# Convolution read from PSUM pairs, a one-engine solver, ordered norm products and separate weight buffers in a two-layer kernel

## The chip, the core and the metric

The kernel runs on one core of a Trainium2 chip. The metric is device time in microseconds (us) of one execution, the median of several. TensorE (PE) multiplies matrices and writes its results to PSUM, which has eight banks of 128 x 512 float32. ScalarE (ACT) and VectorE (DVE) read PSUM and SBUF; in this kernel GpSimd (POOL) works on SBUF alone, and all transfers are issued on the queue of SyncE (SP). Each engine takes its instructions in the order in which they stand in its queue and waits at the first one that is not ready.

## What is computed

Two layers, one after the other, on 1024 tokens of width 1024. The first layer normalizes x, projects it, and runs two branches: neighbourhood attention on a 16 x 64 grid (8 heads of 64), and a gated delta rule in chunks (4 heads of 128, forwards and backwards). The branch of the delta rule begins with a depthwise convolution of five taps over the tokens, and each chunk needs a triangular solve:

```python
qkv = jax.nn.silu(_centred_depthwise_conv(jnp.concatenate([dq, dk, dv], axis=-1), conv_w))
...
a_mat = jnp.where(strict, jnp.einsum('bhncd,bhnsd->bhncs', kb, k) * decay, 0.0) + jnp.eye(C)
sol = lax.linalg.triangular_solve(a_mat, rhs, left_side=True, lower=True, unit_diagonal=True)
...
y = jnp.einsum('ble,ed->bld', jnp.concatenate([attn, delta], axis=-1), w_out)
return x + y
```

The second layer normalizes again and runs stick-breaking attention (8 heads of 128) and a chunked retention (4 heads of 256), merges them through gates, and adds the result to its input.

## The kernel before, in words

Every large product is made three times, with a high and a low part of each operand (`fp32r`): hi x hi, lo x hi, hi x lo. `split_unit` loads 128 rows of a weight matrix into a `raw` buffer and makes the two parts, on POOL (L70 rounds, L71 subtracts), or, with `fast`, for every second unit on ACT (L67) and DVE (L68). `load_units` does so for the eight units of a product; ten `wu` buffers hold them. All units share three `raw` buffers.

PSUM is divided once for the whole program: three accumulators `a` (`psA`) and five banks `z` (two), `t`, `o` and `p` (`psB`). `dense_tok` (L102) makes products of 128 tokens, `dense_col` (L112) products of 128 columns in two accumulators of 512 tokens.

The program is written in this order. **Gates** (L238 to L290): a product for gates and `dz`, then a chain of small operations that ends in a transpose copied out as `growt` (L285). **Delta rule** (L298 to L433), for each of four heads `h`: the weights; for q, k and v (`b`) a `dense_col`, whose accumulators ACT copies to a padded SBUF tile `pad` (L309), after which DVE makes the five taps from `pad` (L312 once, L314 four times) and ACT the silu (L317); norms, transposes and copies (`kt`, `kT`, `vt`); decay matrices `E`; products `pkk` and `pkq`, multiplied by `E` into `N` (L400) and `IT` (L415), and scaled copies `sct` (L424, L428), all written to DRAM. When the last head's `N` is there, `X` (128 systems of 64 x 64, one to a partition) is read back (L433).

**Attention with the solver**: `na_proj(p)` projects q, k, v for a pair of heads (per 128 tokens: squares, a sum, a power on POOL at L126, three copies L495 to L497 on ACT, two scalings L500 on DVE), `na_attn(p)` runs eight steps of scores and values. For p = 0 and 1 the sixteen steps alternate with steps of `solver()`, which goes through 62 columns: for each it multiplies (L457) and adds (L459), on DVE for the rows from 8 up and on POOL for the rows below 8, and on DVE again for the last seven columns. `dz_raw` makes one more projection. For p = 2 the steps alternate with `merges`, which read the solver's result from DRAM; for p = 3 with the scan over chunks.

**Output and second norm**: `out_blocks` (L853) makes the output product in eight blocks of 128 columns for each of two sets of tokens (`s`); `residual` adds x (L860) and `square_sum` collects squares; `normalize(s)` multiplies the eight blocks by the norm (L911), casts (L912) and subtracts (L913). The products of set 0 are taken between the blocks of set 1. Nine `xo` buffers hold the blocks. **Stick-breaking attention** has eight heads with `fast` weights; its tiles lie in the pool `sr`, on the side of SBUF where `hp`, which holds the operand of `out_blocks`, lay.

A pool that is laid over a closed pool waits for all that used the old one. The order within each engine's queue isn't the written one: the builder plans it (`schedule_with_timeline_sim=True`) with its own durations, earlier statements first where both are ready. The order is fixed in the program.

Of the kernel before, what the change touches and what calls it, by code (L numbers as in the profile page):

```python
# [19 lines left out]
P = 128  # L20
# [16 lines left out]
def tile_kernel(ctx: ExitStack, tc: tile.TileContext, I: dict, out: bass.AP, dbg=None, stop=None):  # L37
# [10 lines left out]
    psA = ctx.enter_context(tc.tile_pool(name="psA", bufs=3, space=PSUM))  # L48
    psB = ctx.enter_context(tc.tile_pool(name="psB", bufs=1, space=PSUM))
# [11 lines left out]
    def split_unit(src, ncol, pool=None, tag="wu", parts=1, fast=False, rpool=None):  # L61
        raw = (rpool or wraw).tile([P, ncol], F32, tag="raw", name="raw", bufs=8 if rpool else 3)
# [11 lines left out]
    def load_units(w, c0, width, parts=1, stride=0, pool=None, tag="wu", fast=False, rpool=None):  # L74
        us = []
        for k in range(NK):
            rows = w[k * P:(k + 1) * P, :]
            if parts == 1:
                src = rows[:, c0:c0 + width]
            else:  # L80
                src = rows[:, c0:c0 + parts * stride].rearrange("p (g s) -> p g s", g=parts)[:, :, :width]
            us.append(split_unit(src, width * parts, pool, tag, parts, fast and k % 2 == 1, rpool))
        return us
# [3 lines left out]
    def bank(tag, w=512):  # L87
        if tag == "a":
            return psA.tile([P, w], F32, tag="a", name="acc")
        return psB.tile([P, w], F32, tag=tag, name="p" + tag, bufs=2 if tag == "z" else 1)  # L90
# [16 lines left out]
    def dense_col(hT, us, c0):  # L107
        accs = [bank("a") for _ in range(2)]
# [87 lines left out]


# [55 lines left out]
    onesPP = gp.tile([P, P], F32, name="onesPP")  # L253
    nc.vector.memset(onesPP, 1.0)
    trile = gp.tile([P, P], F32, name="trile")
    trige = gp.tile([P, P], F32, name="trige")
    nc.gpsimd.affine_select(out=trile, in_=onesPP, pattern=[[1, P]], compare_op=ALU.is_ge, fill=0.0, base=0, channel_multiplier=-1)
    nc.gpsimd.affine_select(out=trige, in_=onesPP, pattern=[[-1, P]], compare_op=ALU.is_ge, fill=0.0, base=0, channel_multiplier=1)

# [37 lines left out]
    dc = dc_.__enter__()  # L297
    for h in range(4):  # L298
        kt = dn.tile([P, NM, P], F32, tag="kt", name="kt")
        vt = dn.tile([P, NM, P], F32, tag="sct", name="vt", bufs=2)  # L300
# [3 lines left out]
        for b in range(3):  # L304
            pad = dc.tile([P, T + 4], F32, tag="pad", name="pad", bufs=2)
            nc.gpsimd.memset(pad[:, 0:2], 0.0)
            nc.gpsimd.memset(pad[:, T + 2:T + 4], 0.0)
            for half, acc in enumerate(dense_col(hT, us, b * P)):
                nc.scalar.copy(out=pad[:, 2 + half * 512:2 + half * 512 + 512], in_=acc)  # L309
            cv = dc.tile([P, T], F32, tag="cv", name="cv", bufs=2)  # L310
# [9 lines left out]
        sq = dc.tile([P, T], F32, tag="cv", name="sq", bufs=2)  # L320
# [40 lines left out]
        for d in range(2):  # L361
# [27 lines left out]
            else:  # L389
                E2 = decay(gb, G, 1, True, "E1")  # L390
                nc.vector.tensor_tensor(out=E2, in0=E2, in1=bb, op=ALU.mult)
                for g in range(2):
                    pkk = bank("t")
# [4 lines left out]
                    for dd_, E in enumerate((E0, E2)):  # L398
                        N = dn.tile([P, 4, P], F32, tag="IN", name="N", bufs=2)
# [7 lines left out]
                for g in range(2):  # L407
                    pkq = bank("p")
# [4 lines left out]
                    for dd_, E in enumerate((E0, E1)):  # L413
                        IT = dn.tile([P, 4, P], F32, tag="IN", name="IT", bufs=2)
# [4 lines left out]
        for d in range(2):  # L419
            dh, G = d * 4 + h, Gs[d]  # L420
            nc.scalar.activation(out=G, in_=G, func=AF.Exp)
            for f, src in enumerate((kT, sT[0])):
                sc_t = dn.tile([P, NM, P], F32, tag="sct", name="sct", bufs=2)
# [3 lines left out]
            sc_t = dn.tile([P, NM, P], F32, tag="sct", name="sct", bufs=2)  # L427
# [14 lines left out]

# [932 lines left out]
```

## Time and profile before

| | us |
|---|---|
| median of 3 runs | 2250.16 (2249.15 to 2255.03) |
| the profiled execution | 2252.17 |
| its span, first to last instruction | 2250.5 |
| PE busy | 2163.0 (96%) |
| POOL busy | 1105.4 (49%) |
| DVE busy | 1102.5 (49%) |
| ACT busy | 766.0 (34%) |

A matmul's busy time covers its pipeline, so two neighbours overlap and a busy PE may still wait a little. The profile also has the clock that PE was granted, as a share of full speed; its two levels are 1.2 and 2.4 GHz.

### The profile page before, as it was taken

Reading aid. Unit: us, or ns where it says so; the run is one execution under the profiler, and the core shown is the slowest. Engines: PE = TensorE matmul, PEld = TensorE weight load, DVE = VectorE, ACT = ScalarE, POOL = GpSimd, SP = SyncE. Lnnn points to the kernel's source line nnn. Section 1 sums busy time; section 2 is a strip of 40 time slices with the busy share of each in tenths; the row PEclk is TensorE's granted clock in tenths of the full one; section 3 lists DMA queues with packets and bytes.
Section 4 is the critical chain, followed back from the end, with each engine's and each line's share of the span. In section 5 each row is a group of like instructions: output and inputs, shape, how many; then the busy total and the mean of one; then the engine's idle time right before and its main releaser. Section 6 shows DMA issues by size and latency. Waiting matters only on the chain.

```text
span 2250.5 us, 33410 instructions
## 1 busy us (share of the span) xinstructions
PE 2163.0 (96%) x12325; PEld 1882.8 (84%) x12325; DVE 1102.5 (49%) x1980; ACT 766.0 (34%) x1912; POOL 1105.4 (49%) x1451
## 2 busy tenths in 40 slices
PE   7999888899999999999999999999999999999999
PEld 7777777787889878999999998888988888878887
DVE  4688879953446553566555655123333432231321
ACT  5354433445555322444333433112222322321200
POOL 6667777773101345344333334356565755354532
PEclk9999999899999999999999999999999999999999
DMA  4255740126377542111111112212333323564433
GB/s 132 83 152 157 206 129 26 36 82 190 90 278 246 176 130 63 41 61 57 57 42 34 43 57 71 89 58 79 107 94 120 126 92 114 179 227 159 146 109 106
DMA packets 240196, 250.27 MB, mean 111 GB/s; under 512 B 40161, under 2 KB 175521, under 8 KB 239777
## 3 DMA queue, kind: packets, MB, share of 16 engines
q1 hardware_dynamic: 240032, 248.14, 35.3%
q8 instruction: 97, 1.59, 0.3%
q14 instruction: 67, 0.54, 0.1%
HBM read 172.56 MB, written 75.53 MB: 110 GB/s over the span
## 4 chain that ended last, share of the span: by engine, by line
PE 68%; DVE 11%; POOL 6%; issue 5%; DMA 5%; ACT 2%; SPq 1%; POOLq 0%; DVEq 0%; ACTq 0%
PE acc L112 29%; PE acc L102 17%; PE acc L853 3%; PE po L1083 2%; PE pz L1051 2%; DVE X L459 2%; DVE svt L457 2%; POOL wu L71 2%; DVE cv L314 1%; POOL wu L70 1%; DMA raw<-in_w_in_dram 1%; PE pz L546 1%; PE pt L563 1%; POOL ss L126 1%; PE pp L577 1%
## 5 line engine op out<-in xcount | busy, mean ns | idle before, releaser
L112 PE MATMUL acc<-h2h,wu 128*128 128x512 f32 x1440 | 438.4, 393 | 0.7 <-ACT lg L958 0.7
L102 PE MATMUL acc<-wu,h2h 128*128 128x384 f32 (+1 forms) x1536 | 366.8, 322 | 6.6 <-ACT lg L972 2.2
L71 POOL TENSOR_TENSOR wu<-raw,wu 128x512 fp32r<-128x512 f32 (+3 forms) x276 | 366.3, 1335 | 7.2
L70 POOL TENSOR_SCALAR wu<-raw 128x512 fp32r<-128x512 f32 (+3 forms) x276 | 205.8, 749 | 313.0 <-PE acc L112 202.4
L112 PEld LDWEIGHTS acc<-h2h,wu 128*128 128x128 f32 x1440 | 269.5, 188 | 54.9 <-ACT lg L958 1.1
L102 PEld LDWEIGHTS acc<-wu,h2h 128*128 128x128 f32 x1536 | 265.8, 191 | 11.6 <-ACT lg L972 2.6
L112 PE MATMUL acc<-h2l,wu 128*128 128x512 f32 x720 | 265.2, 392 | 0.0
L102 PE MATMUL acc<-wu,h2l 128*128 128x384 f32 (+1 forms) x768 | 244.9, 321 | 0.0
L102 PE MATMUL acc<-wu,h1hi 128*128 128x384 f32 (+2 forms) x768 | 192.2, 334 | 11.1 <-DVE kS L512 5.2
L112 PE MATMUL acc<-h1hi,wu 128*128 128x512 f32 x512 | 167.3, 416 | 6.8 <-ACT pad L309 3.2
L125 POOL TENSOR_SCALAR ss<-ss 128x2 f32<-128x2 f32 (+2 forms) x136 | 36.7, 270 | 269.6 <-ACT sq L1001 215.0
L112 PEld LDWEIGHTS acc<-h2l,wu 128*128 128x128 f32 x720 | 135.0, 188 | 26.5
L102 PEld LDWEIGHTS acc<-wu,h1hi 128*128 128x128 f32 x768 | 137.0, 195 | 16.0 <-issue 6.5
L102 PEld LDWEIGHTS acc<-wu,h2l 128*128 128x128 f32 x768 | 146.1, 191 | 1.6
L112 PEld LDWEIGHTS acc<-h1hi,wu 128*128 128x128 f32 x512 | 100.4, 198 | 31.8 <-ACT pad L309 4.2
L102 PE MATMUL acc<-wu,h1lo 128*128 128x384 f32 (+2 forms) x384 | 126.7, 333 | 0.0
L126 POOL TENSOR_TENSOR ss<-ss,mhalf 128x2 f32<-128x2 f32 (+2 forms) x136 | 118.9, 875 | 8.3
L112 PE MATMUL acc<-h1lo,wu 128*128 128x512 f32 x256 | 97.9, 411 | 0.0
L1001 ACT ACTIVATE sq<-acc 128x128 f32<-128x128 f32 x128 | 35.5, 286 | 138.7 <-PE acc L102 125.8
L314 DVE SCALAR_TENSOR_TENSOR cv<-pad,c_conv_w,cv 128x1024 f32<-128x1024 f32 x48 | 76.6, 1596 | 1.1
L112 PE MATMUL acc<-oah,wu 128*128 128x512 f32 x256 | 76.1, 393 | 1.0 <-DVE sg L1275 0.6
L102 PEld LDWEIGHTS acc<-wu,h1lo 128*128 128x128 f32 x384 | 74.8, 195 | 0.4 <-issue 0.2
(553 smaller groups left out, 4438.1 us busy)
## 6 DMA issues: line engine op xcount, KB each, us to landing
raw<-in_w_in_dram SPq DMA_DIRECT2D x192, 256.0 KB, 3.0
d_pk<-sct SPq DMA_DIRECT2D x24, 512.0 KB, 4.3
raw<-in_w_out_dram SPq DMA_DIRECT2D x40, 256.0 KB, 3.0
wsa<-d_pk SPq DMA_DIRECT2D x16, 512.0 KB, 6.4
wsb<-d_pk SPq DMA_DIRECT2D x16, 512.0 KB, 7.4
d_sg<-lg SPq DMA_DIRECT2D x32, 256.0 KB, 2.4
sg<-d_sg SPq DMA_DIRECT2D x32, 256.0 KB, 3.4
raw<-in_w_in_dram SPq DMA_DIRECT2D x32, 192.0 KB, 2.8
```

What stands on the lines that cost most here:

```text
L70: nc.gpsimd.tensor_scalar(out=u[:, 0, :], in0=raw, scalar1=1.0, scalar2=0.0, op0=ALU.mult, op1=ALU.add)
L71: nc.gpsimd.tensor_tensor(out=u[:, 1, :], in0=raw, in1=f32(u[:, 0, :]), op=ALU.subtract)
L102: nc.tensor.matmul(acc[:, :n], lhsT=hT[a][:, k, m * P:(m + 1) * P], rhs=us[k][:, b, c0:c0 + n], start=(k == 0 and i == 0), stop=(k == NK - ...
L112: nc.tensor.matmul(accs[half], lhsT=us[k][:, b, c0:c0 + P], rhs=hT[a][:, k, half * 512:(half + 1) * 512], start=(k == 0 and i == 0), stop= ...
L125: nc.gpsimd.tensor_scalar(out=dst, in0=src, scalar1=mul, scalar2=eps, op0=ALU.mult, op1=ALU.add)
L126: nc.gpsimd.tensor_tensor(out=dst, in0=dst, in1=mhalf[:, :eshape], op=ALU.pow)
L314: nc.vector.scalar_tensor_tensor(out=cv, in0=pad[:, i:i + T], scalar=conv_w[:, blk, i:i + 1], in1=cv, op0=ALU.mult, op1=ALU.add)
L457: eng.tensor_tensor(out=tv, in0=X[:, a:a + n, j:j + 1].to_broadcast([P, n, w]), in1=X[:, j:j + 1, j + 1:64].to_broadcast([P, n, w]), op=AL ...
L459: eng.tensor_tensor(out=X[:, a:a + n, j + 1:64], in0=X[:, a:a + n, j + 1:64], in1=tv, op=ALU.add)
L853: nc.tensor.matmul(acc, lhsT=us[k][:, y, (b % 4) * P:(b % 4 + 1) * P], rhs=token_set(mT[x][:, k, 0:T], s), start=(k == 0 and i == 0), stop ...
L1051: nc.tensor.matmul(pz[:, :w], lhsT=qk[0][a][:, i * P:(i + 1) * P], rhs=qk[1][b][:, c0:c0 + w], start=(x == 0), stop=(x == 2))
L1083: nc.tensor.matmul(po[:, i0 * P:512], lhsT=v[a][:, c0 // P + kb, :], rhs=wT[b][:, :n], start=(diag and kb == 0 and x == 0), stop=(diag == ...
```

## The change

1. PSUM is divided three times instead of once. The function `banks` closes the pools and opens new ones: `a` (3) and `z` (2), `t`, `o`, `p` as before, but during the delta rule two pairs `c` of two banks each, and `z`, `t`, `o`, `p` with one bank each.
2. The convolution reads the pair in PSUM: ACT makes the middle tap into `cv` (two instructions), DVE adds the other four taps from the pair. `pad`, its memsets and L312 go. `cv` and `sct` get three buffers, `IN` four; `pkk` and `pkq` alternate between two banks. The masks `trile` and `trige` are made at the start.
3. The solver runs on DVE alone, over all rows, in sixteen equal parts; a part now stands behind the projection's step instead of ahead of it.
4. In `na_proj` the copies of q and k on ACT go; DVE scales from PSUM. The copy `rb` (L587) moves from DVE to ACT.
5. Each norm product of set 0 is ordered on DVE behind the residual block that was written last, and two are taken per block.
6. In stick-breaking attention the units of ACT have two raw buffers `rawf` of their own, in the pool `sr`.

```diff
-    psA = ctx.enter_context(tc.tile_pool(name="psA", bufs=3, space=PSUM))
-    psB = ctx.enter_context(tc.tile_pool(name="psB", bufs=1, space=PSUM))
+    def banks(layout):
+        while ps_pools:
+            ps_pools.pop().__exit__(None, None, None)
+        ps.clear()
+        for i, (tags, bufs) in enumerate(layout):
+            p_ = tc.tile_pool(name="ps" + tags, bufs=bufs, space=PSUM)
...
+    banks((("a", 3), ("ztop", 1)))
...
+        if fast and fpool:
+            raw = fpool.tile([P, ncol], F32, tag="rawf", name="raw", bufs=2)
...
+    def pair():
+        return ps["c"].tile([P, T], F32, tag="c", name="pair")
...
+    banks((("c", 2), ("ztop", 1)))
     for h in range(4):
...
-            for half, acc in enumerate(dense_col(hT, us, b * P)):
-                nc.scalar.copy(out=pad[:, 2 + half * 512:2 + half * 512 + 512], in_=acc)
...
-            nc.vector.tensor_scalar_mul(out=cv, in0=pad[:, 0:T], scalar1=conv_w[:, blk, 0:1])
-            for i in range(1, 5):
-                nc.vector.scalar_tensor_tensor(out=cv, in0=pad[:, i:i + T], scalar=conv_w[:, blk, i:i + 1],
-                                               in1=cv, op0=ALU.mult, op1=ALU.add)
+            acc = pair()
+            dense_col(hT, us, b * P, acc)
+            cv = dc.tile([P, T], F32, tag="cv", name="cv", bufs=3)
+            for half in range(2):
+                hs = slice(half * 512, half * 512 + 512)
+                nc.scalar.activation(out=cv[:, hs], in_=acc[:, hs], func=AF.Copy, scale=conv_w[:, blk, 2:3])
+            for i in (1, 3, 0, 4):
+                a_, b_ = max(0, 2 - i), min(T, T + 2 - i)
+                nc.vector.scalar_tensor_tensor(out=cv[:, a_:b_], in0=acc[:, a_ + i - 2:b_ + i - 2], scalar=conv_w[:, blk, i:i + 1],
+                                               in1=cv[:, a_:b_], op0=ALU.mult, op1=ALU.add)
...
+    banks((("a", 3), ("ztop", 1)))
...
-            if j > LOW:
-                update(nc.vector, tmp, 512, LOW, j, j)
-            update(nc.gpsimd if j >= LOW else nc.vector, tmq, 256, 0, min(j, LOW), j)
-            yield 1
+            for a in range(0, j, step):
+                n = min(step, j - a)
+                tv = tmp[:, :n * w].rearrange("p (r c) -> p r c", r=n)
+                nc.vector.tensor_tensor(out=tv, in0=X[:, a:a + n, j:j + 1].to_broadcast([P, n, w]),
+                                        in1=X[:, j:j + 1, j + 1:64].to_broadcast([P, n, w]), op=ALU.mult)
+                nc.vector.tensor_tensor(out=X[:, a:a + n, j + 1:64], in0=X[:, a:a + n, j + 1:64], in1=tv, op=ALU.add)
+                did += n * w
+                if did * parts >= total * (at + 1):
+                    at += 1
+                    yield 1
...
-            take(sol, 4)
             take(prj, 1)
+            take(sol, 1)
...
+            e = nc.vector.scalar_tensor_tensor(out=xs[k], in0=xs[k], scalar=gain2[:, k:k + 1], in1=rs, op0=ALU.mult, op1=ALU.mult)
+            if s == 0:
+                after(e, turn[0])
...
-            take(norm, 3 if b == 4 else 1)
+            take(norm, 3 if b == 4 else 2)
```

## Rows read from the trace of the kernel before

**Rows 1.** The page, part 1: busy time, share of the span and instructions.
```profile
PE 2163.0 (96%) x12325; PEld 1882.8 (84%) x12325; DVE 1102.5 (49%) x1980; ACT 766.0 (34%) x1912; POOL 1105.4 (49%) x1451
```

**Rows 2.** Windows by stage: length, busy us (instructions) per engine, granted clock, DMA.
```profile
45.00:67.00 22.00, 19.16 (x75) 15.20 (x74) 3.59 (x8) 8.86 (x12) 11.83 (x11) 0.84 0.39 109
67.00:295.00 228.00, 205.20 (x1030) 172.97 (x1028) 182.86 (x180) 100.13 (x207) 162.55 (x148) 0.96 0.58 153
295.00:461.00 166.00, 147.45 (x849) 123.54 (x850) 155.54 (x350) 64.96 (x178) 133.57 (x192) 0.92 0.16 48
461.00:518.00 57.00, 57.00 (x445) 50.12 (x444) 24.11 (x82) 24.95 (x58) 38.30 (x58) 1.00 0.43 124
518.00:650.00 132.00, 124.83 (x1036) 104.91 (x1035) 56.41 (x169) 69.15 (x161) 17.71 (x24) 0.97 0.51 161
790.00:840.00 50.00, 45.62 (x200) 37.44 (x199) 27.95 (x33) 13.97 (x23) 23.33 (x20) 0.93 0.42 133
840.00:912.00 72.00, 68.29 (x355) 62.30 (x354) 26.09 (x49) 19.89 (x64) 35.30 (x50) 0.98 0.28 86
912.00:1400.00 488.00, 483.97 (x2735) 446.06 (x2735) 286.66 (x552) 199.21 (x637) 190.02 (x401) 1.00 0.15 48
```

**Rows 3.** Windows: convolution products, what follows them, and a steady stretch of 512-column matmuls.
```profile
45.00:227.50 182.50, 168.94 (x793) 136.79 (x792) 138.28 (x125) 81.01 (x146) 129.08 (x120) 0.95 0.47 128
227.50:302.00 74.50, 61.64 (x328) 56.31 (x327) 54.72 (x79) 28.96 (x75) 51.48 (x52) 0.91 0.78 198
...
2100.00:2150.00 50.00, 50.00 (x222) 41.45 (x221) 13.66 (x18) 10.67 (x18) 27.41 (x26) 1.00 0.41 132
```

**Rows 4.** Lines of PE, 45 to 227.5 us: busy us, mean ns, idle before, releasers.
```profile
L112 PE MATMUL acc<-h1hi,wu 128*128 128x512 f32 x384 | 124.0, 414 | 6.5 <-ACT pad L309 3.2 <-POOL wu L71 3.1 <-POOL wu L70 0.2
```

**Rows 5.** The chain that ended last, 40 to 70 us: start, duration, what.
```profile
55.74 0.93 DVE graw L275
...
57.78 7.16 PE acc L112 x20
...
65.08 0.29 DVE growt L285
```

**Rows 6.** Single lines: duration in ns, least, median and most; first and last start.
```profile
L314 DVE SCALAR_TENSOR_TENSOR cv<-pad,c_conv_w,cv x48: 1269/1431/3252, 69.3 to 244.5; 128x1024 f32<-128x1024 f32 x48
...
L400 DVE SCALAR_TENSOR_TENSOR N<-pt,E x16: 674/680/692, 117.2 to 275.2; 128x512 f32<-128x512 f32 x16
```

**Rows 7.** Lines of DVE, 295 to 518 us, columns as in rows 4.
```profile
L457 DVE TENSOR_TENSOR svt<-X 128x252 f32<-128x252 f32 (+34 forms) x86 | 54.4, 632 | 4.6 <-DMA X<-d_N 3.0
L459 DVE TENSOR_TENSOR X<-X,svt 128x252 f32<-128x252 f32 (+34 forms) x86 | 54.0, 627 | 1.4
...
L500 DVE TENSOR_TENSOR qn<-qn,ss 128x128 f32<-128x128 f32 x17 | 8.4, 492 | 4.8 <-POOL ss L126 4.6
...
L587 DVE COPY rb<-rs 128x128 f32<-128x128 f32 x15 | 6.6, 437 | 0.1
```

**Rows 8.** DVE in order of time: the solver's start and end [idle before, releaser].
```profile
295.08 0.25 DVE L457 TENSOR_TENSOR svt<-X 128x54 f32<-128x54 f32 x1 [2.97 <-DMA X<-d_N]
...
460.63 0.22 DVE L459 TENSOR_TENSOR X<-X,svt 128x54 f32<-128x54 f32 x1
488.38 0.39 DVE L457 TENSOR_TENSOR svq<-X 128x224 f32<-128x224 f32 x1 [0.89 <-POOL X L459]
488.81 0.39 DVE L459 TENSOR_TENSOR X<-X,svq 128x224 f32<-128x224 f32 x1
```

**Rows 9.** PE in order of time, 806 to 813 us.
```profile
812.27 0.80 PE L853 MATMUL acc<-mahi,wu 128*128 128x512 f32 x1 [4.38 <-DVE xo L860]
```

**Rows 10.** SP's queue and PE in order of time, 836 to 840 us.
```profile
836.74 0.40 PE L853 MATMUL acc<-mdhi,wu 128*128 128x512 f32 x1
...
837.71 0.50 SPq L984 DMA_DIRECT2D gqk<-in_sb_q_gain_dram  x1
```

**Rows 11.** PE in order of time, 903 to 907 us.
```profile
905.91 0.90 PE L102 MATMUL acc<-wu,h2h 128*128 128x384 f32 x2 [2.15 <-ACT lg L972]
```

More of the change, by code (lines that the diff above doesn't have):

```diff
@@ L81, in load_units @@
                 src = rows[:, c0:c0 + parts * stride].rearrange("p (g s) -> p g s", g=parts)[:, :, :width]
-            us.append(split_unit(src, width * parts, pool, tag, parts, fast and k % 2 == 1, rpool))
+            us.append(split_unit(src, width * parts, pool, tag, parts, fast and k % 2 == 1, rpool, fpool))
         return us
@@ L88, in bank @@
         if tag == "a":
-            return psA.tile([P, w], F32, tag="a", name="acc")
-        return psB.tile([P, w], F32, tag=tag, name="p" + tag, bufs=2 if tag == "z" else 1)
+            return ps["a"].tile([P, w], F32, tag="a", name="acc")
+        return ps[tag].tile([P, w], F32, tag=tag, name="p" + tag, bufs=2 if tag == "z" and "a" in ps else 1)
+    def pair():
+        return ps["c"].tile([P, T], F32, tag="c", name="pair")
     def dense_tok(hT, us, c0, n, order=None):
@@ L105, in dense_tok, with dense_col @@
                 yield m, a
-    def dense_col(hT, us, c0):
-        accs = [bank("a") for _ in range(2)]
+    def dense_col(hT, us, c0, acc2=None):
+        accs = [bank("a") for _ in range(2)] if acc2 is None else [acc2[:, 0:512], acc2[:, 512:1024]]
         for k in range(NK):
@@ L195, in tile_kernel @@
     hpp = hp.__enter__()
+    onesPP = sm.tile([P, P], F32, name="onesPP")
+    nc.vector.memset(onesPP, 1.0)
+    trile = sm.tile([P, P], F32, name="trile")
+    trige = sm.tile([P, P], F32, name="trige")
+    nc.gpsimd.affine_select(out=trile, in_=onesPP, pattern=[[1, P]], compare_op=ALU.is_ge, fill=0.0, base=0, channel_multiplier=-1)
+    nc.gpsimd.affine_select(out=trige, in_=onesPP, pattern=[[-1, P]], compare_op=ALU.is_ge, fill=0.0, base=0, channel_multiplier=1)
     hT = join(new_halves("h1", 0), new_halves("h1", 1))
@@ L252, in tile_kernel @@
     gp = gp_.__enter__()
[L253 to L258, printed above, removed]
     gt = gates.rearrange("p m (d c h) -> p d c h m", d=2, c=2)
@@ L318, in tile_kernel @@
             sT.append(s)
-        sq = dc.tile([P, T], F32, tag="cv", name="sq", bufs=2)
+        sq = dc.tile([P, T], F32, tag="cv", name="sq", bufs=3)
         nc.scalar.activation(out=sq, in_=sT[0], func=AF.Square)
@@ L392, in tile_kernel @@
                 for g in range(2):
-                    pkk = bank("t")
+                    pkk = bank("to"[g])
                     for j in range(4):
@@ L407, in tile_kernel @@
                 for g in range(2):
-                    pkq = bank("p")
+                    pkq = bank("pz"[g])
                     for j in range(4):
@@ L586, in values @@
             rb = na.tile([P, 2, 64], F32, tag="rb", name="rb")
-            nc.vector.tensor_copy(out=rb, in_=rs2.unsqueeze(2).to_broadcast([P, 2, 64]))
+            nc.scalar.copy(out=rb, in_=rs2.unsqueeze(2).to_broadcast([P, 2, 64]))
             nc.tensor.transpose(po[:, 2 * P:3 * P], rb.rearrange("p h d -> p (h d)"), ident)
@@ L619, in dz_raw @@
             nc.sync.dma_start(out=d_sz[:, m, 0:256], in_=zt)
-    sol = solver()
-    take(sol, 2)
+    sol = solver(16)
     cur = []
@@ L855, in out_blocks, with after @@
         return accs
+    NOSYNC = mybir.DependencyInfo(mybir.DependencyClass.NoSync, mybir.DependencyReason.DATA)
+    def after(later, earlier):
+        tc.add_manual_dep(later.ins, earlier.ins.name, NOSYNC, reason="engine order")
+    turn = [None]
     def residual(pool, tag, bufs, acc, s, b):
@@ L943, in tile_kernel @@
         return
-    NOSYNC = mybir.DependencyInfo(mybir.DependencyClass.NoSync, mybir.DependencyReason.DATA)
-    def after(later, earlier):
-        tc.add_manual_dep(later.ins, earlier.ins.name, NOSYNC, reason="table order")
     d_sg = dram.tile([16, P, T], F32, name="d_sg")
```

59 lines of the change are left out of this document (26 added, 33 removed).

## The prediction

> **What bounds the kernel now.** First the page's totals: PE is busy for 2163.0 of the span's 2250.5 us, every other engine for half or less [rows 1]. So only time in which PE stands, or runs at its lower level (1.2 of 2.4 GHz), can be won. Next the windows by stage [rows 2]: a stage's loss is its length less PE's busy time, plus (1 − granted clock) times its length. That gives 6.4 us for 45 to 67, 22.8 + 9.1 = 31.9 for 67 to 295 (delta rule), 18.5 + 13.3 = 31.8 for 295 to 461 and 0 for 461 to 518 (attention with the solver), 11 for 518 to 650, 7.9 for 790 to 840, 5.2 for 840 to 912. From 912 on PE is busy nearly throughout at full clock. The change touches the stages that hold some 80 us of loss; that is the most it can give.
>
> Then the delta rule alone. Its 576 convolution matmuls lie between 45 and 227.5; at the cadence of a steady stretch, 50/222 = 0.225 us, they need 130 us, and the 217 short ones some 24, of 182.5 [rows 3]. PE's releasers there come to 6.5 us, half ACT's copy to `pad`, half POOL's weights [rows 4]; the rest of the loss is clock and short gaps. From 227.5 to 302 nothing of the convolution is left: 12.9 idle, 6.7 clock, though `na_proj(0)` already fills holes [rows 3]. This tail, in which DVE works off what it owes, is the costliest part.
>
> Last the solver. It starts at 295.1, when `X` is read back; DVE has done its rows at 460.6 and waits until 488.4 for POOL's [rows 8]. In 295 to 518 DVE is busy for 155.5 + 24.1 = 179.6 us, POOL for 171.9 [rows 2].
>
> **The convolution.** Removed: per block L312 once and L314 four times. L314 takes 1.269 to 3.252 us, mean 1.60, so 48 x 1.60 = 77, and L312 about 12; its slow cases lie where POOL runs. An operation of the same form with its input in PSUM, L400, takes 0.674 to 0.692 at 512 columns, never more [rows 6]. No row has 1024 columns from PSUM: the upper bound is 2 x 0.68 = 1.36, the lower one 1.21 (0.166 fixed and 1.0 ns per element, the price worked out below from rows 8, gives 1.19). I take 1.25: 48 x 1.25 = 60. DVE gains 77 + 12 − 60 = 28 of 138 us. ACT's 24 copies become scaled ones, perhaps 0.1 us each, hidden: ACT is busy for 81 of 182.5 [rows 3].
>
> The Trainium skill speaks against this edit ("VectorE: DVE Perf Modes", section "Rules for kernel authors"): where several operations are done on a matmul's output, copy it to SBUF first, or accept the slow rate from PSUM. By that the taps would be no cheaper than from `pad`. The row disagrees: L400 from PSUM takes 0.68, as 512 elements cost by the solver's price from SBUF, and does not stretch.
>
> Against it stands what a pair holds up. Before, PE was freed by one copy per half; now a pair is held through ACT's 1.4 us and four taps, some 6.5 us, against 16 x 3 x 0.225 = 10.8 us of matmuls per block. With two pairs DVE has slack within a head. At its end DVE has some 21 us of other work for that head (norms, `N`, `IT`); if the plan puts it ahead of the next taps, both pairs fill and PE waits. I take 12 us for the three changes of head, bounds 5 and 30.
>
> **The start.** The pairs lie over the old accumulators and over `ztop`'s bank. If a pool waits for all that used the old one, no convolution matmul can begin before `growt` is copied out, at 65.1; ahead of that copy's matmuls 20 convolution matmuls stood, 7.16 us, so it moves to about 59 [rows 5]. That the wait is of whole pools I read from `gqk`: it lies in the pool `sr` over `hp` and is issued at 837.7, one microsecond after the last matmul that reads from `hp` [rows 10]. Lost: 36 early and those 20 matmuls, 56 x 0.23 = 12.9; regained 6.3; the clock falls there, 2 to 3; but the 3.3 us that PE waits for POOL's weights later [rows 4], with the low clock that follows, are taken up. Net −3, bounds −10 and +1.
>
> **End of the delta rule.** So PE ends the convolution near 227 as before, but DVE owes less: 28 us over the stage, of which I let about 12 reach the reading of `X` (283 for 295), since the last head's chain of transposes, writes and reads stays. `z` has one bank until then, so `na_proj(0)` no longer fills holes, about 6 us. Attention begins near 297 for 302.
>
> **The solver.** From rows 8 an instruction of 54 elements takes 0.22 us and one of 224 takes 0.39: 1.0 ns per element and 0.166 fixed. Before, DVE's part is 172 instructions of some 0.63, 108.4 us [rows 7], and the last columns, 122 in all, 92 by that price: a stretch of 1.3 beside POOL's solver. After: 212 instructions over 2 x 41,664 elements, 83.3 + 35.2 = 118.5, and 0.04 between them, 127 us. POOL loses its 93 us of solver out of 172 and keeps the weights, so I take a stretch of 1.13, bounds 1.0 and 1.3: 143 us (127 to 163), 21 more than before. Gone from DVE: `rb` 6.6 us [rows 7], which ACT takes with its 65 of 166 busy [rows 2] as cover, and some 4 us of L500's wait for POOL's `ss`, now with PSUM as source. DVE comes to 179.6 + 21 − 6.6 − 4 = 190.
>
> Before, DVE ran at 155.5/166 = 94% while the solver was on, 15 steps of it, and then waited 28 us for POOL. Now nothing waits for POOL: 190/0.937 = 203 us, so attention runs from 297 to 500 where it ended at 518. PE's own floor is 223 − 32 = 191 us, so 488 is the best. I take 17 us for delta rule and attention together, bounds −5 and +37 (start at its worst and stretch 1.3; both at their best with PE at its floor).
>
> **The norm.** At 807.5 PE waits 4.38 us for a residual L860 [rows 9], because products L911 and L913 of set 0 stood ahead of it on DVE, and the clock falls: the window 790 to 840 lost 7.9 [rows 2]. The new order puts each product behind a residual, two per block; the DVE has 22 of 50 us free, so what is queued behind a product waits for 1 us at most. Gain 7, bounds 0 (if the tile of x, with nine `xo`, comes late anyway) and 8.
>
> **Stick-breaking attention.** `rawf` lies in `sr`, so ScalarE's first weights can be loaded only after 836.7, where before they came into the common buffers earlier: a new wait of PE at the start, 4 us, bounds 0 and 6. In return ACT's `lg` at 903 no longer stands behind a rounding that waits for its load: 2.15 idle [rows 11] and the low clock after it, most of the 5.2 us lost in 840 to 912 [rows 2]. I take +1, bounds −4 and +5.
>
> **Nothing in the sum.** The masks are made while the first weights load; three `cv`, four `IN` and the banks of `pkk` only loosen waits. If POOL were full where the masks are made, they would cost about 1 us.
>
> **Sum.** 17 + 7 + 1 = 25. The profiled execution took 2252.2, 2 above the median 2250.2, so 2227 in its own terms and **2225** for the median.
>
> **Rivals.**
> (B) The larger gain. DVE paces neither stage: pairs never fill, the stretch is 1.0, attention runs near PE's floor and ends at 480 to 488. For it: the 28 us that DVE sheds. Against it: DVE stays at nearly 190 of 203. Time: 30 to 37 and 8 to 20, so 2195 to 2212. It also holds if the wait is by bank, so that nothing is lost at the start (+10).
> (C) Nothing much moves. The solver's stretch stays 1.3 although POOL's solver is gone, DVE comes to 210 and attention lasts 223 as before, and the start eats what the convolution gives; only the norm is won: 2243 to 2250, and to 2256 if `rawf` costs its 6.
> (D) Slower, by one mechanism: the hold of pairs at a change of head. If both pairs are full when DVE begins the head's last work, PE stands until that work (21 us) and one block's taps (5 us) are through, less what is still to be filled, one pair's 10.8 at the most: 15 to 21 us, three times, and 2 to 3 us at half clock behind each, 52 to 70 in the place of my 12. 25 − 40 to 25 − 58 is a loss of 15 to 33: 2265 to 2283. It decides once a change of head holds both pairs for longer than the 10.8 us of one block; the queues are planned with other durations than the chip's, so no row excludes it. Against it: DVE was idle for 44 us of that stretch [rows 3] and sheds 28 more.
> (E) The change does not do what it says: the taps from PSUM stretch like those from `pad`. It speaks against this that L400 never did [rows 6]; its time lies in (C) or (D).
>
> **How the numbers follow.** Forecast (2212 to 2243) 0.5; B 0.2; C 0.15; D 0.15, with E inside C and D. 0.3%, 6.75 us, is about what a measurement of this kernel can tell from no change: faster begins under 2243.4, slower above 2256.9. Faster: 0.5 + 0.2 + a little of C = 0.72; same: the rest of C, 0.13; slower: D, 0.15. The range runs from B's lower end, 2195, to 2270, a quarter into D: that leaves out some 0.11 above and a little below.
>
> **What would show it.** The taps' line with least and most close to each other at 1.2 to 1.3; first convolution matmul at 59, not 45; PE's idle time under that line put down to DVE `cv` or not (D); `X` read back near 283; L457 and L459 at about 0.5 us with the whole near 143, and no wait of DVE for POOL's X; the end of attention at about 500; no gap of 4 us near 807; a new gap just behind 837 ended by POOL or ACT weights, none at 903. The prediction is wrong if PE waits for `cv` for over 25 us, or if the solver's steps delay those of attention so that PE's loss from 297 to 500 exceeds 30.

## The result and the profile after

The changed kernel takes 2263.33 us (median of 4 runs, 2261.24 to 2265.33) where the kernel before took 2249.65 beside it: a ratio of 1.0068 with a 95% interval of 1.005 to 1.0086, some 15 us slower. The forecast was 25 us faster, with 2270 as the upper end of its range. Its sign was wrong, and none of its rivals names the main cause.

The first look is at the totals of the page and at the windows by stage, in the columns of [rows 1] and [rows 2].

```profile
PE 2161.3 (96%) x12325; PEld 1887.8 (83%) x12325; DVE 1074.6 (48%) x1956; ACT 764.4 (34%) x1878; POOL 985.7 (44%) x1271
```

```profile
45.00:67.00 22.00, 9.71 (x40) 7.77 (x39) 4.87 (x11) 10.55 (x15) 12.62 (x12) 0.69 0.34 94
67.00:295.00 228.00, 205.72 (x1043) 178.34 (x1042) 146.81 (x174) 95.32 (x187) 120.14 (x120) 0.94 0.60 160
295.00:461.00 166.00, 150.26 (x889) 126.54 (x889) 153.38 (x337) 65.34 (x159) 63.48 (x68) 0.94 0.13 41
790.00:840.00 50.00, 45.89 (x207) 37.36 (x207) 28.65 (x35) 13.36 (x22) 19.35 (x19) 0.98 0.41 130
840.00:912.00 72.00, 60.28 (x300) 55.27 (x299) 28.19 (x44) 18.45 (x61) 38.44 (x48) 0.90 0.23 69
```

DVE lost 28 us of work and GpSimd 120, as the change says, and PE lost nothing: it does the same matmuls, in a longer span. Its loss (length less busy time, and the missing share of the clock) grew where the change touched it: from 6.4 to 12.3 + 6.8 = 19.1 in 45 to 67, from 31.9 to 22.3 + 13.7 = 36.0 in the delta rule, and from 5.2 to 11.7 + 7.2 = 18.9 in 840 to 912. In attention it fell, from 31.8 to 15.7 + 10.0 = 25.7. This measure, which is also the forecast's, counts a time twice in which PE stands and its clock is low as well; it compares stages, but its terms can't be added up to a loss in time.

To see what of this stays, each matmul's start is compared with the start of the same matmul before (median over those of a stretch of 25 us). PE is 10 us late at 75, level with before at 150 to 200 (1 to 2 early), 10 late at 225, 11 late at 350, level again from 400 to 790 (within 1 us but for a stretch of 2 to 4 around 575), 5 early at 825, 13 late at 850, 9 late from 903 on, 11 to 12 late from 1700 to the end. (The two profiled spans, 2261.8 and 2250.5, are 11 us apart; the medians are some 15.) Differences of a few us that grow slowly say little here: before_rawf, an experiment below, has the same matmuls as before in the same order up to 838, and drifts 5 us ahead of it by then. A step at one place says more.

So the delta rule and attention, which were to give 17 us, gave nothing; the norm gave nearly 6; and between the last output product at 831.5 and 870 PE lost 18 us, of which 4 came back at 903. About 6 of the 18 are lost by 851.33, at waits for the first loads of the stage, and about 12 in one stop behind it. That stop is the largest part of the result. PE, columns as in [rows 9], the changed kernel and then the kernel before, and windows of the changed kernel around the stop:

```profile
851.33 0.34 PE L122 MATMUL acc<-wu,h2l 128*128 128x384 f32 x1
863.39 0.98 PE L122 MATMUL acc<-wu,h2h 128*128 128x384 f32 x2 [11.72 <-DVE sq L1026]
```

```profile
852.07 0.58 PE L102 MATMUL acc<-wu,h2h 128*128 128x384 f32 x2 [1.56 <-DVE sq L1007]
```

```profile
831.00:849.00 18.00, 14.48 (x78) 13.87 (x78) 9.76 (x13) 5.97 (x10) 11.88 (x12) 0.91 0.46 138
849.00:878.00 29.00, 17.28 (x75) 15.56 (x74) 14.01 (x21) 6.62 (x27) 20.89 (x28) 0.76 0.24 73
851.00:863.40 12.40, 0.68 (x5) 0.39 (x4) 9.00 (x12) 3.27 (x14) 12.10 (x16) 0.66 0.13 41
863.40:868.40 5.00, 5.00 (x16) 5.00 (x17) 2.10 (x6) 1.26 (x6) 4.76 (x9) 0.50 0.38 110
```

PE stands for 11.7 us and then works at half its clock for 5 us. The clock falls while it stands: of the 7 us of clock that miss in 849 to 878 (29 x 0.24), 4.2 (12.4 x 0.34) lie in the stop itself. PE waits for an accumulator that DVE reads in L1026 with a factor `ss`. ScalarE makes `ss` as a sum of squares of that accumulator, and GpSimd computes its power in two steps, L145 and L146. GpSimd's queue in the changed kernel shows why that is late:

```profile
821.25 1.70 POOL L937 TENSOR_TENSOR h2l<-xo,h2h 128x512 fp32r<-128x512 f32 x1 [1.28 <-ACT h2h L936]
837.04 0.20 POOL L145 TENSOR_SCALAR rt__8178<-rt__8178 128x4 f32<-128x4 f32 x1 [14.08 <-DVE rt__8178 L922]
837.32 0.62 POOL L87 TENSOR_SCALAR wu<-raw 128x512 fp32r<-128x512 f32 x1
...
859.45 0.19 POOL L145 TENSOR_SCALAR ss<-ss 128x2 f32<-128x2 f32 x1
...
861.88 1.39 POOL L146 TENSOR_TENSOR ss<-ss,mhalf 128x2 f32<-128x2 f32 x2
```

And in the kernel before:

```profile
849.28 0.19 POOL L125 TENSOR_SCALAR ss<-ss 128x2 f32<-128x2 f32 x1
...
850.31 0.20 POOL L125 TENSOR_SCALAR rt__8423<-rt__8423 128x4 f32<-128x4 f32 x1
850.58 0.70 POOL L126 TENSOR_TENSOR ss<-ss,mhalf 128x2 f32<-128x2 f32 x1
...
861.17 3.47 POOL L913 TENSOR_TENSOR h2l<-xo,h2h 128x512 fp32r<-128x512 f32 x2 [0.17 <-ACT h2h L912]
```

GpSimd stands for 14 us at `rt`, the power of the second norm's sums, with the weights of the next products behind it. From 837 to 859 it works without a pause: weights, the subtractions L937 of the second norm, more weights; only then comes `ss`. In the kernel before `rt` and the subtractions (L913) stood behind those weights and behind the first `ss`, whose power was done at 851.3, and PE waited 1.6 us at this place.

GpSimd isn't the only engine with another order. DVE's eight products of the second norm for set 1 and ScalarE's casts of them have moved ahead of this accumulator as well, so that ScalarE comes to its squares 8 us later than before. First the changed kernel, then the kernel before:

```profile
843.91 9.89 DVE L933 SCALAR_TENSOR_TENSOR xo<-xo,c_norm_gain,rs 128x512 f32<-128x512 f32 x8
852.67 0.27 ACT L1020 ACTIVATE sq<-acc 128x128 f32<-128x128 f32 x1
```

```profile
844.97 0.28 ACT L1001 ACTIVATE sq<-acc 128x128 f32<-128x128 f32 x1 [4.09 <-PE acc L102]
859.69 8.54 DVE L911 SCALAR_TENSOR_TENSOR xo<-xo,c_norm_gain,rs 128x512 f32<-128x512 f32 x8
```

So the second norm's work on set 1 stands ahead of the first accumulators of the next stage. GpSimd, which has no pause from 837 on, comes to `ss` last, 6 us after the squares are there, and sets the end of the stop. Nothing in the statements that these three engines execute here was changed but the raw buffers of some weights and the norm's order for the other set. The order of their queues was.

### The profile page after: what moved, and what is told of

Its sections match the earlier page's. It is cut to its first block, busy times and chain, and to the rows that moved or that the text cites. A ratio compares the mean times of both kernels' runs of the same rounds, so it can differ in the third digit from the quotient of the medians.

```text
span 2261.8 us, 33117 instructions
## 1 busy us (share of the span) xinstructions
PE 2161.3 (96%) x12325; PEld 1887.8 (83%) x12325; DVE 1074.6 (48%) x1956; ACT 764.4 (34%) x1878; POOL 985.7 (44%) x1271
## 4 chain that ended last, share of the span: by engine, by line
PE 74%; DVE 7%; POOL 6%; DMA 5%; issue 5%; ACT 2%; SPq 1%; POOLq 0%; DVEq 0%; ACTq 0%
PE acc L132 28%; PE acc L122 19%; PE pair L132 4%; PE acc L868 3%; PE po L1102 2%; PE pz L1070 2%; POOL wu L88 2%; POOL wu L87 2%; DVE svt L478 2%; DVE X L480 1%; PE pz L562 1%; DMA raw<-in_w_in_dram 1%; PE pt L579 1%; PE acc L988 1%; DMA G<-d_g 1%
## 5 line engine op out<-in xcount | busy, mean ns | idle before, releaser
L122 PE MATMUL acc<-wu,h2h 128*128 128x384 f32 (+1 forms) x1536 | 369.3, 324 | 15.9 <-DVE sq L1026 11.7
L88 POOL TENSOR_TENSOR wu<-raw,wu 128x512 fp32r<-128x512 f32 (+3 forms) x276 | 356.2, 1300 | 8.3
L87 POOL TENSOR_SCALAR wu<-raw 128x512 fp32r<-128x512 f32 (+3 forms) x276 | 194.3, 707 | 325.6 <-PE acc L132 231.8
L145 POOL TENSOR_SCALAR ss<-ss 128x2 f32<-128x2 f32 (+2 forms) x136 | 34.7, 255 | 387.9 <-ACT sq L1020 241.2
L146 POOL TENSOR_TENSOR ss<-ss,mhalf 128x2 f32<-128x2 f32 (+2 forms) x136 | 119.7, 881 | 9.2
L132 PE MATMUL pair<-h1hi,wu 128*128 128x512 f32 x384 | 110.6, 404 | 0.8 <-DVE growt L305 0.5
L132 PEld LDWEIGHTS pair<-h1hi,wu 128*128 128x128 f32 x384 | 72.7, 193 | 17.0 <-issue 0.7
L478 DVE TENSOR_TENSOR svt<-X 128x440 f32<-128x440 f32 (+38 forms) x106 | 72.3, 682 | 9.8 <-DMA d_pk<-IT 7.9
L132 PE MATMUL acc<-obh,wu 128*128 128x512 f32 x256 | 74.9, 389 | 0.0
```

Of the source, the lines that this page charges most:

```text
L87: nc.gpsimd.tensor_scalar(out=u[:, 0, :], in0=raw, scalar1=1.0, scalar2=0.0, op0=ALU.mult, op1=ALU.add)
L88: nc.gpsimd.tensor_tensor(out=u[:, 1, :], in0=raw, in1=f32(u[:, 0, :]), op=ALU.subtract)
L122: nc.tensor.matmul(acc[:, :n], lhsT=hT[a][:, k, m * P:(m + 1) * P], rhs=us[k][:, b, c0:c0 + n], start=(k == 0 and i == 0), stop=(k == NK - ...
L132: nc.tensor.matmul(accs[half], lhsT=us[k][:, b, c0:c0 + P], rhs=hT[a][:, k, half * 512:(half + 1) * 512], start=(k == 0 and i == 0), stop= ...
L145: nc.gpsimd.tensor_scalar(out=dst, in0=src, scalar1=mul, scalar2=eps, op0=ALU.mult, op1=ALU.add)
L146: nc.gpsimd.tensor_tensor(out=dst, in0=dst, in1=mhalf[:, :eshape], op=ALU.pow)
```

## The experiments

Ratios are to the kernel before, run beside each (0.1% is 2.2 us); intervals are at 95%. Two ratios that differ by less than about 0.2% aren't told apart.

| kernel | us | ratio | interval |
|---|---|---|---|
| the change | 2263.3 | 1.0068 | 1.005 to 1.0086 |
| before_rawf | 2263.7 | 1.0077 | 1.0055 to 1.0098 |
| after_norawf | 2244.5 | 0.9989 | 0.9976 to 1.0003 |
| after_rawf1 | 2244.3 | 0.9985 | 0.9972 to 0.9998 |
| before_norm | 2245.2 | 0.9987 | 0.9975 to 1.0 |
| before_conv | 2260.7 | 1.0052 | 1.0033 to 1.0071 |
| before_solver | 2252.7 | 1.0014 | 1.0003 to 1.0025 |
| rawf1_start | 2241.7 | 0.9975 | 0.9961 to 0.9989 |
| after_three | 2243.3 | 0.9977 | 0.9964 to 0.999 |
| start_last2 | 2236.6 | 0.9946 | 0.993 to 0.9963 |
| start_all | 2262.6 | 1.0068 | 1.0043 to 1.0093 |
| rawf1_oldsolver | 2251.1 | 1.002 | 1.0003 to 1.0037 |
| noconv_rawf1 | 2246.5 | 0.9991 | 0.9978 to 1.0003 |
| conv_start_last2 | 2242.2 | 0.9975 | 0.9963 to 0.9988 |
| start_last2_pqt | 2237.4 | 0.9949 | 0.9933 to 0.9964 |

### Which part made the stop at 851

Two parts of the change meet there: the separate raw buffers in `sr` and the new order of the norm. The first kernel takes the buffers away, the second takes them away for the first head alone, the third and fourth put the one and the other on the kernel before.

```diff
-            us = load_units(I["w_in_2"], 128 * h, 128, parts=4, stride=1024, fast=True, fpool=sr)
+            us = load_units(I["w_in_2"], 128 * h, 128, parts=4, stride=1024, fast=True)
```

> The changed kernel with the common raw buffers for ScalarE's weights again; the rest of the change stays. Theory W (the weights): the two buffers in the pool sr cost PE 17 us at the start of stick-breaking attention (its instructions stand 3.8 us earlier than before at 831 and 12.8 later at 864) and give 3.7 back at 903; without them the time falls by 13, from 2263 to about 2250, and the stop of 11.7 us at 851 is gone. Rival N (the norm): the stop comes from the new order of the norm products, which brings work of the second set onto DVE and GpSimd too early; then the time stays at 2263 and the stop stays.

```diff
-            us = load_units(I["w_in_2"], 128 * h, 128, parts=4, stride=1024, fast=True, fpool=sr)
+            us = load_units(I["w_in_2"], 128 * h, 128, parts=4, stride=1024, fast=True, fpool=sr if h else None)
```

> The changed kernel with the separate raw buffers only from the second head of stick-breaking attention on; the first head loads into the common ones. Theory W: the stop at 851 goes as without the separate buffers, but ScalarE's wait near 903 stays away, so 3 to 4 us less than that kernel: 2246. Rival N: 2263.

The kernel before with `fpool` as in the change:

> The kernel before with nothing changed but the separate raw buffers in the pool sr. Theory W: about 13 us slower than before, 2263, with a stop of 10 to 14 us of PE some 15 us after the last output product, and GpSimd standing before that at the norm's power of the second set with the weights behind it. Rival N: no difference, or 3 us faster.

The kernel before with `after(e, turn[0])` and two products per block as in the change:

> The kernel before with nothing changed but the order of the norm products of the first set. Theory W: 4 to 5 us faster, about 2245, as the gap of 4.4 us near 807 goes with part of the half clock after it. Rival N: slower, up to 2262.

Theory W holds for the stop on all four. Without the buffers the stop is gone and the time falls by 0.8%; the buffers alone cost 0.77%, 17 us, as much as the whole change. In that kernel GpSimd stands at `rt` as in the changed one, and PE stops at the same place:

```profile
838.13 0.20 POOL L128 TENSOR_SCALAR rt__8423<-rt__8423 128x4 f32<-128x4 f32 x1 [17.87 <-DVE rt__8423 L903]
```

```profile
864.65 0.98 PE L105 MATMUL acc<-wu,h2h 128*128 128x384 f32 x2 [12.36 <-DVE sq L1010]
```

The order of GpSimd's queue has `rt` ahead of the weights in the two kernels whose first head loads into `sr`, and behind most of them in the kernel before, in after_norawf, after_rawf1 and before_norm. The queues are planned; a unit whose buffer lies over `hp` is planned late, so what used to stand behind the weights is put ahead of them. That the planner reasons so was read from these orders, not from the planner. That the buffers make the stop is shown; that they make it by the order of the queues is read from the traces, since no run keeps the buffers and restores the order.

With the buffers from the second head on, the first head's stop is gone and ScalarE's wait near 903 doesn't come back in the trace (it does in after_norawf, where PE waits 2.1 us for `lg`), but the two times are the same within their intervals, where theory W expected 3 to 4 us. The norm's order alone gives 0.13%; in its window PE is idle for 1.7 us in the place of 4.4 [rows 2], and the clock doesn't fall:

```profile
790.00:840.00 50.00, 48.26 (x224) 39.93 (x223) 30.34 (x36) 14.50 (x24) 25.84 (x20) 1.00 0.46 145
```

### Where the 17 us of delta rule and attention went

First the two parts alone on the kernel before: convolution, bank pairs, masks and buffer counts in the one, solver, projection and `rb` in the other.

> The kernel before with the convolution's part of the change alone (bank pairs, taps from PSUM, masks at the start, the larger counts of cv, sct and IN). Theory L (lost at two waits): DVE's relief is real, some 20 us, and is eaten by two waits for a bank: 10 us at the start, where PE stands from 46 to 57.8, and 12 us at 226, where the norm's sums of the last head wait for the only bank z; total 0, within 5 us, with both stops in the trace. Theory A (absorbed): the stops cost nothing in the end because attention is bound by something else that begins when X is read; total 0 too, but then the shift against before, some +10 behind the stop at 226, is still there at 295 and gone only in attention, where DVE's solver, not PE, sets the pace.

> The kernel before with the solver on DVE alone, the scalings of q and k from PSUM and the copy rb on ScalarE. Theory L: the solver does not set attention's end, PE has work enough beside it: 0, within 4 us. Theory A: DVE's order sets it, and the time moves with DVE's sum in attention (190 for 180 us, or less by the wait for GpSimd): faster by 5 to 10 or slower by 5 to 10.

The convolution's part costs 0.52% alone, against both theories; the solver's 0.14%, 3 us, inside the 4 of theory L. The stops that theory L named are in the trace of the first (11.5 us at 45, 11.4 at 227). Then both stops were attacked on the kernel with separate buffers from the second head on.

```diff
-    banks((("a", 3), ("ztop", 1)))
+    banks((("a", 3), ("z", 1), ("top", 1)))
...
-    pg = bank("z")
+    pg = bank("p")
...
-    pgt = bank("z")
+    pgt = bank("p")
```

> The changed kernel with separate raw buffers from the second head on, and with the first division of PSUM made of three pools (a, z, top), the gates' products in top, so that the pairs lie over banks that are free at about 46. Theory L: the convolution begins at 46 and the 10 us of the start come back, 2234 against 2244 for the same kernel without this. Theory A: the start comes back and is lost again at 226 or in attention; 2244. If the wait at the start is by bank and not by pool the convolution would have begun at 46 in any order, and nothing changes.

The same, and in the delta rule:

```diff
-        pq = bank("z")
+        pq = bank("t")
```

> As the kernel with the split first division, and with the sums of the delta rule's norm in bank t in the place of z. Theory L: both stops go, 18 to 22 us less than the changed kernel with raw buffers from the second head on: 2222 to 2228. Theory A: 2240 to 2246.

The first division decides when the convolution begins: at 46.68 in the place of 60.04. The run changes two things, the division and the bank of the gates' products. That the wait was for whole pools follows if the first pair lies over two old accumulators, as the order of the pools has it: by this run they are free at 46.68, and in the changed kernel the pair waited for `growt` all the same. But at 79.7 PE waits 4.1 us for DVE's taps, and of the 10 us, 5 are left at 700 by the starts of the matmuls; the times differ by 0.10%, within the uncertainty, so theory L's first half isn't borne out in the time. The stop at the end stayed:

```profile
235.26 3.54 PE L345 MATMUL pz<-ones,sq 128*128 128x2 f32 x16 [11.47 <-DVE IT L436]
```

With the sums in another bank it stayed too, with another releaser, and behind it the wait that counts:

```profile
235.68 3.57 PE L345 MATMUL pt<-ones,sq 128*128 128x2 f32 x16 [7.91 <-ACT sq L342]
244.88 0.98 PE L122 MATMUL acc<-wu,h1hi 128*128 128x384 f32 x2 [4.48 <-DVE cv L335]
```

So theory L's second half fell: the bank `z` was only what stood first in PE's queue. `na_proj(0)`, which filled this time before [rows 3], has accumulators that lie over the pairs, and the pairs are held until DVE's last tap. That gave theory H, and a kernel that copies the last two blocks out (the accumulators come free with ScalarE's copy), and one that does it for all blocks.

```diff
             dense_col(hT, us, b * P, acc)
             cv = dc.tile([P, T], F32, tag="cv", name="cv", bufs=3)
+            if h == 3 and b > 0:
+                pd = dc.tile([P, T], F32, tag="pd", name="pd", bufs=2)
+                for half in range(2):
+                    hs = slice(half * 512, half * 512 + 512)
+                    nc.scalar.copy(out=pd[:, hs], in_=acc[:, hs])
+                acc = pd
```

> The kernel with the split first division and separate raw buffers from the second head on; in addition the last two blocks of the convolution (head 3, b = 1 and 2) are copied out of their pairs by ScalarE, and their taps read the copy. Theory H (hold at the end): PE stands from 224 to 235 and runs at half clock for 17 us after it because na_proj(0)'s accumulators lie over the pairs and these are held until DVE's last tap; with the copy na_proj(0) begins within 3 us of the last convolution product, and the time falls by 8 to 15, to 2227 to 2234. Rival K (chain): na_proj(0) only begins earlier and then waits for the read of X or for DVE, as later in attention; 2240 to 2243.

> The same with the copy for all twelve blocks: no tap reads PSUM, DVE's taps cost again what they cost from SBUF (1.4 to 1.6 us in the place of 1.2), and no pair is held longer than ScalarE needs. If DVE's relief in the convolution is worth what the prediction took from it (12 us of the read of X), this is 10 us slower than the kernel with two copied blocks; if only the hold of the banks matters (theory H), within 4 us of it.

With two blocks copied `na_proj(0)` begins at 226.41, right behind the convolution, and the kernel is 0.29% faster than without the copy, 0.54% faster than the kernel before. The gain, 5 to 6 us, is less than the 8 to 15 expected: PE then stands 6.3 us at 245.6 for `z` and 9.0 us at 290.6 for DVE. (Of the 17 us at half clock that the expectation counts behind the stop, 8 lie in it: the clock falls at 227.) And it is won although `X` is read 12 us later than in the changed kernel:

```profile
226.41 0.60 PE L122 MATMUL acc<-wu,h1hi 128*128 128x384 f32 x2
```

```profile
302.95 0.50 DVE L484 TENSOR_TENSOR svt<-X 128x62 f32<-128x62 f32 x1 [11.98 <-DMA X<-d_N]
```

Copying all blocks is 26 us slower than copying two, where theory H expected no difference and its rival 10. The taps cost 1.42 us in the median and up to 2.76 there, but this isn't the main loss: `pkk` of the last head, on which `N` and `X` depend, is queued on PE behind `na_proj(0)`, DVE waits for it, and `X` comes at 333; PE, ahead until then, stands 16.9 us at 335.

```profile
311.55 1.29 DVE L427 SCALAR_TENSOR_TENSOR N<-po,E 128x512 f32<-128x512 f32 x2 [8.13 <-PE po L423]
...
333.37 0.26 DVE L484 TENSOR_TENSOR svt<-X 128x62 f32<-128x62 f32 x1 [10.46 <-DMA raw<-in_w_in_dram]
```

What the taps alone are worth can't be read from this kernel.

### Does each part pay by itself

The old solver in the changed kernel (with separate buffers from the second head on), and the old convolution in it:

> The changed kernel with separate raw buffers from the second head on, and the solver of the kernel before (rows below 8 on GpSimd, parts ahead of the projection's). Alone on the kernel before, the convolution's part cost 12 us and the solver's 3, and yet both together with the norm cost nothing. Theory J (joint): the convolution's part pays only with the solver on DVE: 2255 to 2258. Theory S (each its own): the solver moves nothing in attention, where PE sets the pace: 2241 to 2247.

> The changed kernel without the convolution's part (accumulators and taps as before), with separate raw buffers from the second head on. Theory J: 2244 to 2249, since what the convolution costs and gives cancel when the solver is on DVE. Theory S: 12 us less than with the convolution, 2232.

The solver on DVE is worth 0.35% where the convolution reads pairs, and cost 0.14% where it doesn't; the convolution's part is worth 0.06% with the rest, which is nothing that can be told, and cost 0.52% alone. So the parts don't add; theory J expected that, with 2255 to 2258 where 2251 was measured, between its range and that of theory S. The last two runs ask how much of the convolution's cost is the two holds, and whether `z` is a third: the convolution's part alone with both cured, and the fastest kernel with the sums in bank `t`.

> The kernel before with the convolution's part alone, and with both holds cured (first division in three pools, last two blocks copied out of their pairs). Theory H (the holds are the whole cost of that part): from 12 us slower to 0 to 4 us faster than before, 2244 to 2248. Theory J (the rest of the cost lies in attention and goes only with the solver on DVE): still 4 to 8 us slower than before, 2251 to 2255.

> The kernel with both holds cured, and the sums of the delta rule's norm in bank t in the place of z. With both cured PE still stood from 239.0 to 245.6 at these sums, behind DVE's last reading of z, and ran at half clock for 10 us. If z is a third hold: 5 to 9 us less than 2236.6. If the sums only wait for their input as well (the chain of the last block): the same within 3 us.

With both holds cured the convolution's part alone goes from 0.52% slower to 0.25% faster, 17 us, a little more than theory H asked. So curing the holds takes away the whole cost of that part, and with them gone it doesn't need the solver. (Each of these edits also has the queues planned anew; how much of the 17 us that is, no run tells.) `z` is no third hold: the time is the same, and PE's stop has moved to 224, where it waits 6.4 us for ScalarE's copies. Why the solver on DVE takes up the cost of the holds where they are, wasn't settled, but the windows behind the convolution show where to look. The first is of before_solver, which has no pairs, the second of before_conv, the third of conv_start_last2:

```profile
227.50:302.00 74.50, 50.87 (x283) 46.89 (x282) 50.67 (x83) 25.84 (x61) 43.97 (x39) 0.86 0.80 211
227.50:302.00 74.50, 57.15 (x307) 53.71 (x308) 46.89 (x79) 26.33 (x71) 40.68 (x53) 0.86 0.81 210
227.50:302.00 74.50, 62.45 (x337) 59.09 (x336) 42.75 (x68) 28.16 (x74) 49.88 (x48) 0.89 0.74 192
```

PE is idle there for 23.6 us with the solver's part alone, for 17.4 with the convolution's alone, for 12.1 with its holds cured, and was for 12.9 before [rows 3]. So the solver's part by itself makes PE stand at the end of the delta rule, for 7.0 us at 258 and 7.5 us at 296.5, and the changed kernel, idle for 20.5, stands no longer there than before_solver does without any pair:

```profile
258.35 1.11 PE L349 MATMUL po<-ident,kt 128*128 128x128 f32 x4 [7.01 <-DVE kt L340]
296.54 0.69 PE L525 MATMUL po<-ident,qd 128*128 128x128 f32 x2 [7.52 <-ACT qd L522]
```

The course of attention is the solver's too: PE is 11 us late at 350 and level at 400 in the changed kernel as in before_solver.

The version that beats both kernels is start_last2: 2236.6 us, 0.54% less than before (0.37 to 0.70) and 1.2% less than the change.

## Why the prediction was wrong, point by point

**Stick-breaking attention, the step that failed first.** The forecast had the buffers wait for `hp`, 4 us at the start, 4 back at 903, +1 in all with −4 as the worst. By the starts of the matmuls it was −14. The wait is there: `gqk`, the first load into `sr`, is issued at 831.96, as in [rows 10] just behind the last product that reads `hp`, and PE stands 2.2 us at 835.7 for the second norm's sums and 1.3 us at 838.1 for ScalarE's weights. That start cost about 6 us, the top of the bounds of 0 to 6, and the 3.7 us at 903 came. What was left out is the queues around the moved loads: a load that lands later moves in the planned order, and the second norm's work on set 1 was put ahead of the first accumulators on GpSimd, ScalarE and DVE. That is the stop at 851, 11.7 us standing and 5 us of work at half clock against 1.6 and none at the same matmuls before, about 12 us in time. The bound was taken from the wait of the moved loads alone; the work queued around them was never priced, though the trace of before shows GpSimd at work between 838 and 861 with hardly a pause.

**The measure of loss.** The first step of the forecast counts a stage's loss as PE's idle time plus its missing clock. Where the clock is low while PE stands, as in 851 to 863.4 above, this counts the same time twice, so "some 80 us" was more than could be won.

**The taps, right.** 1.25 was forecast with 1.21 and 1.36 as bounds:

```profile
L335 DVE SCALAR_TENSOR_TENSOR cv<-pair,c_conv_w,cv x48: 1266/1281/1284, 74.2 to 237.8; 128x1023 f32<-128x1023 f32 x24, 128x1022 f32<-128x1022 f32 x24
```

No tap is stretched, where L314 went to 3.25 [rows 6]. DVE's work in 45 to 227.5 fell from 138.3 [rows 3] to 111.9, 26 for the 28 forecast. The Trainium skill's advice for elementwise work on a matmul's output ("VectorE: DVE Perf Modes", section "Rules for kernel authors"), to accept the 1x rate from PSUM or to copy it to SBUF first if many operations follow, finds no price here: the least that a tap took from SBUF was 1.269 [rows 6], and from PSUM 1.266. What the reading from PSUM cost here is the bank that it holds.

**The start, right.** The first convolution product begins at 60.04 (59 forecast), behind `growt`, for whole pools:

```profile
57.80 0.60 PE L299 MATMUL pz<-graw,trile 128*128 128x32 f32 x2 [11.51 <-POOL wu L88]
...
60.04 1.19 PE L132 MATMUL pair<-h1hi,wu 128*128 128x512 f32 x2 [0.47 <-DVE growt L305]
```

(The releaser named is an old one; PE has nothing to do until `graw` is ready.) The cure was worth 0.10%, against the net 3 us of the forecast.

**Changes of head, better than forecast, and the end, worse.** 12 us were set for three changes of head; PE waited 0.3 us for a pair at 149.8 and 3.2 us for `z` at 192.9. Rival D's mechanism, DVE doing a head's last work between the taps of blocks that wait, came at the one place where nothing stood behind: after the last block. The four taps of one block lie at 227.5, 229.9, 233.8 and 237.8 with the third head's work between them. The forecast had "about 6 us" there, since `na_proj(0)` no longer fills holes; the window, against 12.9 + 6.7 in [rows 3], shows 20.5 + 13.4:

```profile
227.50:302.00 74.50, 53.96 (x284) 51.06 (x285) 46.67 (x84) 24.35 (x58) 33.80 (x35) 0.82 0.80 208
```

That is 7.6 us more idle time and 6.7 us more of missing clock. The term was mis-sized, but the hold is not its only cause: before_solver, without pairs, is idle there for 23.6 us (shown above), and no term of the forecast had the solver's part cost anything at this place.

**Solver and attention: the numbers right, the step from them wrong.** The 212 instructions, forecast at 143 us with the gaps between them, take 72.3 + 67.9 = 140.2 without; the solver ends at 494 where about 500 was forecast.

```profile
L478 DVE TENSOR_TENSOR svt<-X 128x440 f32<-128x440 f32 (+38 forms) x106 | 72.3, 682 | 9.8 <-DMA d_pk<-IT 7.9
L480 DVE TENSOR_TENSOR X<-X,svt 128x440 f32<-128x440 f32 (+38 forms) x106 | 67.9, 640 | 2.0
```

But PE's last value product of the second pair begins at 526.6, before at 526.7; of the first pair at 422.5 and 423.9. The forecast took the solver's end for the end of the stage, though [rows 2] showed PE full from 461 to 518: an engine that ends earlier than one that is full brings nothing. start_last2 shows the same from the other side: its solver ends at 508, 14 us later, and its last value product of the second pair begins at 520.4, 6 us earlier. `X`, read at 290.9 for 283 forecast, was not the path either. The 6 us less that PE loses in 295 to 461 only make good what the end of the delta rule cost; before_solver has both, 16.5 us idle in 295 to 461 for 18.5 before, and 23.6 for 12.9 ahead of it.

**The norm, right in kind.** The gap at 807 is gone, and by the starts of the matmuls PE gains 5.8 us across it, for 7 forecast and within its bounds. The part alone gave 0.13%.

**In all.** 25 us were forecast as 17 + 7 + 1. By the starts of the matmuls it was 0 + 6 − 14, and some 2 more lost later, no more than two profiles differ by themselves. The two signs that were to show the prediction wrong didn't come: PE waited 0.3 us for `cv`, not 25, and its loss from 297 to 500 was 15.4 + 10.2 = 25.5, under 30. Both watched the stages that the forecast thought of. The rivals priced a hold of pairs, DVE's speed and the start; none priced a changed order on engines whose statements didn't change.

## What to carry to other kernels

When buffers move to another pool, ask not only when their loads can start, but which queue works on them and what else stands in that queue: where the order is planned, a late load can reorder the work around it, and an accumulator may be freed by the engines that were reordered. Reading an accumulator many times in place saves a copy but holds the bank; count the holds at the ends of the stage, where the next stage's work can't start in those banks, and copy out just there. And the end of a helper's work is the end of a stage only if PE is idle at that time.

## What the runs showed that was not expected

Parts of a change don't add where queues are planned: convolution, solver, norm and buffers alone come to +0.52, +0.14, −0.13 and +0.77%, together 1.30%, and the change is at +0.68%. And reading an accumulator in place cost more than it gave until two waits for banks were cured: with them the convolution's part alone is 0.52% slower than before, without them 0.25% faster.
